# A hybrid mixer layer on one core: the last 512 columns of the second token tile in two halves, epsilon as a summand, the last stores over two queues

## The chip, the cores and the metric

The kernel runs on one core of a Trainium2 chip. What is measured is the device time of one execution in microseconds (us). The engines are named as in the profile: PE does the matrix products (PEld is its weight load), DVE the elementwise work on tensors, ACT the activations, POOL is the general-purpose engine, and SP issues transfers. A "q" behind a name (SPq, ACTq) marks what the engine's sequencer does, such as issuing a transfer.

## The reference

One layer on 256 tokens of 2048 features, all in float32. What matters here is its end:

```python
    gate = jax.nn.sigmoid(rmsnorm(x, ple_norm_g[i]) @ w_ple_gate[i])
    x = x + gate * (p[i] @ w_ple_proj[i])

return rmsnorm(x, final_norm_g)
```

with `rmsnorm(x, g) = x * rsqrt(mean(x * x) + EPS) * g` over the 2048 features of a token. Before it come the projection of the normalised input into ten fields, a short convolution and a gated recurrence on them, their merge, and an output projection that is added to x. The final norm needs the squares of all 2048 features of a token before any of them can be written.

## The kernel before

**Products.** Every weight matrix comes as a stream of chunks of 256 rows by 512 columns. SP loads them (L104), ACT rounds each to a first part (L117) and DVE subtracts to get the rest (L118), so that three products (L796 to L798) make up one of float32's accuracy. A group is 512 output columns; PE goes through its k tiles of 128 rows, and for each through both tiles of 128 tokens (`NT` = 2). The result of a group and a token tile fills one PSUM bank of 128 x 512.

**Order.** One list of steps (`steps`) gives the order of the chunks. After each step `advance()` moves every open epilogue, a Python generator, to its next `yield`; so the code of an epilogue stands in program order between the products of later steps. Each engine works through its own instructions in order, and a scheduler may set independent neighbours differently: of two halves, the two sigmoids come before the two squares on ACT. Semaphores carry the waits between engines. The last eight groups alternate between the per-layer embedding (`PP`, 2 k tiles) and the gate (`PG`, 16 k tiles), ending with a gate group. `ep_pg` (L596) handles the first three gate groups: sigmoid on ACT, product and sum on DVE, then on ACT the square with its sum over the columns (`accum_out`) into a column of `ss3`; POOL multiplies the result by the final gain.

**The last group.** It is written out by hand (L853 to L867). By then all its chunks are split or nearly so, so it is done by token tiles: all 48 products of tile 0 (16 k tiles, three products each), then all 48 of tile 1. `ep_last` for tile 0 runs beside tile 1's products; `ep_last` for tile 1 runs after everything.

**`ep_last` (L616)** takes the bank's 512 columns in two halves of 256: sigmoid (L624), times the embedding's part (L627), sum into x (L630), square with its sum (L631, which ends with an instruction that reads the accumulator out). Then DVE adds up the five sums of the token tile (L635), divides by 2048 and adds epsilon (L159), and POOL raises to the power -1/2 (L163). The four groups of columns are then scaled, two on ACT (L643, columns 0 to 1023) and two on DVE (L645, L647), and SP issues a store of 256 KB for each as it is ready (L650).

At the end the program waits for the transfers and the engines (L938).

Of the kernel before, what the change touches and what calls it, by code (L numbers as in the profile page):

```python
# [17 lines left out]
T = 256          # tokens  # L18
NT = T // P      # token tiles
D = 2048  # L20
KT = D // P      # k tiles of D
DC = 1024        # conv width
DR = 1024        # recurrent width
NH = 8           # heads
CW = 512         # columns of a product group
# [5 lines left out]
SCAN = 64        # tokens between restarts of the running sum of log f  # L31
LEVELS = [128, 64, 32, 16, 8, 4]      # block sizes inside a 128-token tile; pairs come apart

# columns of W_in in the order in which they are computed, in groups of 512
# [4 lines left out]
# columns of the packed per-feature parameters  # L39
# [5 lines left out]
def hybrid_kernel(ctx, tc, xT, x, pT, prm, gfin, masks, w_in, w_a, w_b, w_o, w_pg, w_pp, out):  # L45
# [8 lines left out]
    # what lives for a part of the kernel: by name, the pool and what closes it  # L54
# [32 lines left out]
    # ---------------------------------------------------------------- weights  # L87
    # a weight [groups of 512 columns, P, chunks of two k tiles, 2 * CW] comes as a stream of chunks
    stream = []                   # (weights, group, chunk)
    loaded = {}                   # raw tiles by (id, group, pair of chunks)  # L90
    parts = {}                    # split tiles by position in the stream
# [30 lines left out]
    # -------------------------------------------------------------- constants  # L122
# [16 lines left out]
    def operand(pool, tag, n):  # L139
        """n k tiles of a stationary operand, x^T-like: [P, n, T] in two parts."""  # L140
        return tuple(pool.tile([P, n, T], F32R, tag=tag + x, bufs=1, name=nm(tag + x)) for x in "hl")

    def put(op, k, src, scale=None):
        """src (fp32, [P, n]) times a per-partition gain into k tiles of an operand, as two parts."""
        hi, lo = op[0][:, k, :], op[1][:, k, :]
        if scale is None:
            nc.scalar.activation(out=hi, in_=src, func=AF.Copy)
            nc.vector.tensor_tensor(out=lo, in0=src, in1=hi.bitcast(F32), op=ALU.subtract)
        else:
            nc.scalar.activation(out=hi, in_=src, func=AF.Identity, scale=scale)  # L150
            nc.vector.scalar_tensor_tensor(
                out=lo, in0=src, scalar=scale, in1=hi.bitcast(F32), op0=ALU.mult, op1=ALU.subtract
            )

    # ----------------------------------------------------------- small pieces
    def rsqrt_of(ss, n, width, tag):
        """(ss / width + EPS) ** -0.5 for [P, n]."""
        v = sc(n, tag + "v", 2)
        nc.vector.tensor_scalar(  # L159
            out=v, in0=ss, scalar1=1.0 / width, scalar2=EPS, op0=ALU.mult, op1=ALU.add  # L160
        )
        r = sc(n, tag + "r", 2)
        nc.gpsimd.tensor_tensor(out=r, in0=v, in1=mhalf[:, :n], op=ALU.pow)  # L163
        return r

    def transposed(src):
        """src [P, NT, 512] token-major -> two PSUM banks, each [P, 2, T] (two column tiles)."""
        banks = []
        for half in range(2):
            b = bank("s")  # L170
            for i in range(2):
                c = half * 2 + i
                for t in range(NT):
                    nc.tensor.transpose(  # L174
                        b[:, i * T + t * P : i * T + (t + 1) * P],
                        src[:, t * CW + c * P : t * CW + (c + 1) * P],
                        ident,
                    )
            banks.append(b)
        return banks  # L180

    # --------------------------------------------------- epilogues, GEMM 1
# [14 lines left out]
    def times(psum, other, dst):  # L197
        """dst = (psum * rstd) * other"""
# [7 lines left out]
    def segments(ap):  # L206
        """[P, 1024] -> [P, head, tile of 128 tokens, segment, SCAN]"""
        return ap.rearrange("p (h k s c) -> p h k s c", h=4, k=2, c=SCAN)

    def ep_f(j, psum):  # L210
# [24 lines left out]
        # running sum of log f by position: with its own token in tile 0 (in time's order), and  # L235
        # without it in tile 1 (in the reverse order), restarting every SCAN tokens
# [51 lines left out]
    def hgrn(j):  # L288
        """
        The recurrence of four heads as masked products A[s, t] of two tiles of 128 tokens. Tile 1 is in  # L290
        the reverse order of time, so that at every level the keys of tile 0 lie where the queries of
        tile 1 do: one product serves both, A of tile 0 above the diagonal and A of tile 1 below it.
        """
# [27 lines left out]
        def tiles(ap, B):  # L321
            """[P, 1024] -> [P, head, tile, block of B, half, B / 2]"""
            return ap.rearrange("p (h k n two c) -> p h k n two c", h=4, k=2, two=2, c=B // 2)

        def combine(e, B):
            """The keys and the queries of a level, scaled by e."""
# [13 lines left out]
        def level(B):  # L340
            """By the decay between each token and the middle of its block of B."""
# [15 lines left out]
        # from the end of a segment, y = b - its sum  # L357
# [17 lines left out]
        # between the two tiles of 128 tokens  # L375
# [13 lines left out]
        # pairs of tokens and each token with itself: f of the later one on its query, 1 / f on its key  # L389
# [75 lines left out]
    def ep_xa(j, psum):  # L465
# [7 lines left out]
        for h in range(2):  # L473
            for i in range(2):
# [9 lines left out]
                # tokens 0 .. 127 in time's order, then tokens 255 .. 128  # L484
# [46 lines left out]
    # --------------------------------------------------- epilogues, the rest  # L531
# [64 lines left out]
    def ep_pg(j, psum):  # L596
        xs, pw, gt = state["x"], state["pw", j], t4()
        junk = t4()
        for t in range(NT):
# [9 lines left out]
                accum_out=state["ss3"][:, t * 5 + j : t * 5 + j + 1],  # L609
# [6 lines left out]
    def ep_last(t, psum):  # L616
        """The last 512 columns of a tile of tokens, its norm and its way out."""
        xs, pw, ss = state["x"], state["pw", 3], state["ss3"]
        n = 256
        gt, junk = t4(), t4()  # L620
        for h in range(2):
            s = slice(h * n, (h + 1) * n)
            d = xs[:, t, 3 * CW + h * n : 3 * CW + (h + 1) * n]
            nc.scalar.activation(  # L624
                out=gt[:, s], in_=psum[:, s], func=AF.Sigmoid, scale=state["rstd2"][:, t : t + 1]
            )
            nc.vector.tensor_tensor(  # L627
                out=gt[:, s], in0=gt[:, s], in1=pw[:, t * CW + h * n : t * CW + (h + 1) * n], op=ALU.mult
            )
            nc.vector.tensor_tensor(out=d, in0=d, in1=gt[:, s], op=ALU.add)  # L630
            nc.scalar.activation(  # L631
                out=junk[:, s], in_=d, func=AF.Square, accum_out=ss[:, t * 5 + 3 + h : t * 5 + 4 + h]
            )
        tot = sc(1, "tot3", 2)
        nc.vector.tensor_reduce(  # L635
            out=tot, in_=ss[:, t * 5 : (t + 1) * 5], axis=mybir.AxisListType.X, op=ALU.add
        )
        r = rsqrt_of(tot, 1, D, "r3")
        for q in (0, 2, 3, 1):
# [10 lines left out]
            nc.sync.dma_start(out=out[:, t, s], in_=d)  # L650
        yield

    # ------------------------------------------------------------ the program
# [4 lines left out]
    groups = []                   # (kind, j, weights, group in it, operand's name)  # L658
# [17 lines left out]
    # x^T and the first weights, in the order in which they are needed  # L676
# [15 lines left out]
    # a busy tensor engine runs at its full clock by the time the data is there  # L692
# [10 lines left out]
    def add_squares(c):  # L703
        """Towards the norm of x: squares summed over the k tiles, and in norm_of_x over the partitions."""
# [23 lines left out]
    def begin():  # L728
        """The lower bound of the forget gate, and what is needed later."""
        # softmax over the layers (one), its running sum, less the first  # L730
# [17 lines left out]
    def second_part():  # L748
        """The mixer's temporaries go; m^T comes."""
# [6 lines left out]
    def third_part():  # L756
        """The branches' outputs go; the residual stream comes back."""
# [18 lines left out]
        state["ss3"] = sc(10, "ss3", 1)  # L776
# [12 lines left out]
    def ahead(pos):  # L789
        """How many chunks are split by the time that one is used: all of the last group's at its start."""  # L790
        return LEAD + min(max(pos - (last_group - 8), 0), 5)

    def product(psum, op, k, t, hi, lo, first, last):
        """Three products make up one of float32's accuracy."""
# [58 lines left out]
    # the last group by tiles of tokens: the first one's end overlaps the second one's products  # L853
    for t in range(NT):
        bk = bank("g")
        for c in range(len(steps) - last_group):
# [4 lines left out]
            for i in range(2):  # L861
                k = 2 * c + i
                s = slice(i * CW, (i + 1) * CW)
                product(bk, state["x1T"], k, t, hi[:, s], lo[:, s], k == 0, k == KT - 1)
            if c % 2:
                advance()
        active.append(ep_last(t, bk))  # L867
# [6 lines left out]
def _chunks(w):  # L874
    """[K, N] -> [N / 512, 128, K / 256, 2 * 512]: row (2 c + i) * 128 + p of a group at [p, c, i]."""
# [5 lines left out]
def _features(v):  # L881
    """[n * 128] -> [128, n]"""
# [3 lines left out]
def _level_masks():  # L886
    """The pairs of each level, for both tiles; all of them, by tile; the pairs left over, by tile."""
# [7 lines left out]
def _in_order(v):  # L895
    """[T, n]: the second tile of tokens reversed (its own inverse)."""
# [46 lines left out]
```

## Time and profile before

| What | us |
|---|---|
| Three runs | 865.38, 866.03, 867.37 |
| Median | 866.03 |
| Span of the profiled execution | 864.5 |
| Time of the profiled execution beside its span | not given by the page |
| PE busy | 847.6 |
| Tile 1's products, first start | 844.3 |
| Tile 1's sigmoid | 855.5 |
| First scaling of tile 1 | 859.1 |
| First and last issue of its stores | 859.6, 861.0 |

A row of the page's fifth part names a line, an engine, an operation, its output and inputs, the shape and how often; then the busy time and the mean of one in ns, and the idle time ahead of it with what ended most of it. In the timeline the first two numbers are the start from the span's beginning and the duration, both in us; instructions of one group that follow each other stand in one row (x2), and the bracket tells the idle time ahead and its cause. Products overlap in the array, so the distance between the starts of two, not their duration, is what one costs. The view by stretches gives, for each, its length, the busy time and count of PE, PEld, DVE, ACT and POOL, the granted clock of PE, the busy share of the 16 DMA engines (which can come out a little above 1) and the GB/s moved.

### The profile page before, as it was taken

What the parts mean: (1) busy time and instruction counts of PE and PEld (TensorE: products, weight loads), DVE (VectorE), ACT (ScalarE), POOL (GpSimd) and SP (SyncE); (2) the same over time, 40 slices, a digit from 0 to 9 for tenths busy, and PEclk for the clock granted to TensorE, in tenths of its full rate; (3) what the DMA queues carried; (4) which work ended last, traced back from release to release, by engine and by line L of the source; (5) the groups of instructions that cost most, each with busy time, mean ns of one, the idle gap of its engine ahead of it and who ended that gap; (6) DMA issues with size and microseconds to landing.
All of it is one profiled execution on the core that took longest, in us unless ns stands there. A gap on an engine that the chain in (4) does not pass through costs nothing.

```text
span 864.5 us, 9830 instructions
## 1 busy us (share of the span) xinstructions
PE 847.6 (98%) x3853; PEld 697.8 (81%) x3853; DVE 535.0 (62%) x613; ACT 423.7 (49%) x514; POOL 94.3 (11%) x81
## 2 busy tenths in 40 slices
PE   8799999999999999999999999999999999999995
PEld 5588888888888888888888888888888888888884
DVE  7684586986674586976546447446446555555572
ACT  7474474444654573444444443444443544455552
POOL 3310032302010041302001001001001000001110
PEclk9999999999999999999999999999999999999999
DMA  9455545454455455454555555554554955454542
GB/s 337 181 194 196 195 160 181 149 194 159 181 186 176 174 195 195 147 181 160 181 193 191 172 193 194 191 195 171 197 192 172 354 191 195 172 187 165 207 147 97
DMA packets 25390, 162.02 MB, mean 187 GB/s; under 512 B 2944, under 2 KB 2944, under 8 KB 7168
## 3 DMA queue, kind: packets, MB, share of 16 engines
q1 hardware_dynamic: 25200, 161.36, 52.7%
q8 instruction: 30, 0.49, 0.2%
q14 instruction: 16, 0.13, 0.0%
q10 hardware_dynamic: 144, 0.04, 0.0%
HBM read 159.29 MB, written 2.10 MB: 187 GB/s over the span
## 4 chain that ended last, share of the span: by engine, by line
PE 93%; issue 2%; ACT 2%; DMA 1%; POOL 0%; SPq 0%; DVE 0%; POOLq 0%; ACTq 0%
PE g L796 30%; PE g L798 30%; PE g L797 29%; PE s L306 1%; PE s L174 1%; ACT whi L117 1%; DMA raw<-in_w_in 1%; ACT xh L150 0%; PE s L414 0%; PE s L572 0%; ACT t L712 0%; PE s L425 0%; PE s L426 0%; PE s L427 0%; POOL r1r L163 0%
## 5 line engine op out<-in xcount | busy, mean ns | idle before, releaser
L118 DVE TENSOR_TENSOR wlo<-raw,whi 128x1024 fp32r<-128x1024 f32 (+1 forms) x294 | 373.3, 1275 | 273.2 <-ACT whi L117 272.9
L117 ACT ACTIVATE whi<-raw 128x1024 fp32r<-128x1024 f32 (+1 forms) x294 | 308.6, 1052 | 375.1 <-PE g L798 366.6
L796 PE MATMUL g<-whi,xh 128*128 128x512 f32 x896 | 355.8, 398 | 0.8 <-ACT whi L117 0.8
L797 PE MATMUL g<-wlo,xh 128*128 128x512 f32 x896 | 350.7, 391 | 5.3 <-DVE wlo L118 5.3
L798 PE MATMUL g<-whi,xl 128*128 128x512 f32 x896 | 352.2, 393 | 0.0
L797 PEld LDWEIGHTS g<-wlo,xh 128*128 128x128 f32 x896 | 169.0, 189 | 43.1 <-DVE wlo L118 7.3
L798 PEld LDWEIGHTS g<-whi,xl 128*128 128x128 f32 x896 | 168.9, 189 | 38.0
L796 PEld LDWEIGHTS g<-whi,xh 128*128 128x128 f32 x896 | 169.1, 189 | 35.9 <-ACT whi L117 2.2
L796 PE MATMUL g<-whi,mh 128*128 128x512 f32 x128 | 50.8, 397 | 0.0
L798 PE MATMUL g<-whi,ml 128*128 128x512 f32 x128 | 50.2, 392 | 0.0
L797 PE MATMUL g<-wlo,mh 128*128 128x512 f32 x128 | 49.8, 389 | 0.0
L544 POOL TENSOR_TENSOR gb<-ga,gb 128x1024 f32<-128x1024 f32 x4 | 9.6, 2406 | 259.9 <-DVE gb L543 259.9
L334 POOL TENSOR_TENSOR X<-t,kT 128x256 f32<-128x256 f32 x12 | 11.4, 952 | 170.9 <-ACT t L348 117.1
L798 PEld LDWEIGHTS g<-whi,ml 128*128 128x128 f32 x128 | 24.0, 188 | 5.6
L797 PEld LDWEIGHTS g<-wlo,mh 128*128 128x128 f32 x128 | 24.1, 188 | 5.1
L796 PEld LDWEIGHTS g<-whi,mh 128*128 128x128 f32 x128 | 24.1, 188 | 4.7
L796 PE MATMUL g<-whi,yaTh 128*128 128x512 f32 x64 | 24.9, 390 | 0.0
L798 PE MATMUL g<-whi,yaTl 128*128 128x512 f32 x64 | 24.9, 390 | 0.0
L797 PE MATMUL g<-wlo,yaTh 128*128 128x512 f32 x64 | 24.9, 389 | 0.0
L796 PE MATMUL g<-whi,ybTh 128*128 128x512 f32 x64 | 24.9, 389 | 0.0
L797 PE MATMUL g<-wlo,ybTh 128*128 128x512 f32 x64 | 24.9, 389 | 0.0
L798 PE MATMUL g<-whi,ybTl 128*128 128x512 f32 x64 | 24.9, 389 | 0.0
(155 smaller groups left out, 579.0 us busy)
## 6 DMA issues: line engine op xcount, KB each, us to landing
raw<-in_w_in SPq DMA_DIRECT2D x91, 1024.0 KB, 4.8
raw<-in_w_o SPq DMA_DIRECT2D x16, 1024.0 KB, 4.8
raw<-in_w_pg SPq DMA_DIRECT2D x16, 1024.0 KB, 4.8
raw<-in_w_a SPq DMA_DIRECT2D x8, 1024.0 KB, 5.0
raw<-in_w_b SPq DMA_DIRECT2D x8, 1024.0 KB, 5.0
raw<-in_w_in SPq DMA_DIRECT2D x9, 512.0 KB, 7.8
t<-in_xT SPq DMA_DIRECT2D x8, 256.0 KB, 7.5
xs<-in_x SPq DMA_DIRECT2D x2, 1024.0 KB, 8.7
```

Source lines behind the costliest of these rows:

```text
L117: nc.scalar.activation(out=hi[:, s], in_=src[:, s], func=AF.Copy)
L118: nc.vector.tensor_tensor(out=lo[:, s], in0=src[:, s], in1=hi[:, s].bitcast(F32), op=ALU.subtract)
L174: nc.tensor.transpose(b[:, i * T + t * P : i * T + (t + 1) * P], src[:, t * CW + c * P : t * CW + (c + 1) * P], ident,)
L306: nc.tensor.matmul(bk[:, s], X[:, 0, h, :], X[:, 1, h, :], start=True, stop=True)
L334: eng.tensor_tensor(out=xv[:, w, :, :, half, :], in0=ev[:, :, blk, :, half, :], in1=src[:, :, blk, :, half, :], op=ALU.mult,)
L544: nc.gpsimd.tensor_tensor(out=gb, in0=ga, in1=gb, op=ALU.add)
L796: nc.tensor.matmul(psum, oh, hi, start=first, stop=False)
L797: nc.tensor.matmul(psum, oh, lo, start=False, stop=False)
L798: nc.tensor.matmul(psum, ol, hi, start=False, stop=last)
```

## The change

The last group is done in three pieces instead of two: tile 0 with 512 columns, then tile 1 with columns 0 to 255 of the group over all 16 k tiles, then with columns 256 to 511. Each piece has a bank of its own. The epilogue of a half (`last_half`) is put behind that half's products, so tile 1's first half is dealt with in program order before the second half's products are through; the norm (`last_norm`) comes after both. The sigmoid's tile also takes the squares that nobody reads.

The division by 2048 goes into the squares, as the activation's input scale, in `ep_pg` and in `last_half`. Each token tile has six summands instead of five; the sixth is epsilon, written once by POOL. L159's instruction goes from this norm, and POOL takes the power of the sum itself. In program order the sixth summand is set in `third_part`; in the order that the scheduler makes of it, it stands among POOL's first instructions.

Of the last stores, the one of columns 512 to 1023 is issued by ACT, the other three by SP. The scalings are written in the order 2, 0, 3, 1 instead of 0, 2, 3, 1; the stores on SP stood in the order 2, 0, 3, 1 before already.

Up to the last group, the instructions of all engines keep their order, but for the setting of epsilon.

```diff
@@ ep_pg
             nc.scalar.activation(
                 out=junk[:, s], in_=d, func=AF.Square,
-                accum_out=state["ss3"][:, t * 5 + j : t * 5 + j + 1],
+                scale=D**-0.5, accum_out=state["ss3"][:, t * 6 + j : t * 6 + j + 1],
             )
@@
-    def ep_last(t, psum):
...
+    def last_half(t, h, psum):
+        xs, pw, ss, n = state["x"], state["pw", 3], state["ss3"], CW // 2
+        gt = t4()[:, :n]
+        d = xs[:, t, 3 * CW + h * n : 3 * CW + (h + 1) * n]
+        nc.scalar.activation(out=gt, in_=psum, func=AF.Sigmoid, scale=state["rstd2"][:, t : t + 1])
+        nc.vector.tensor_tensor(
+            out=gt, in0=gt, in1=pw[:, t * CW + h * n : t * CW + (h + 1) * n], op=ALU.mult
+        )
+        nc.vector.tensor_tensor(out=d, in0=d, in1=gt, op=ALU.add)
+        nc.scalar.activation(
+            out=gt, in_=d, func=AF.Square, scale=D**-0.5,
+            accum_out=ss[:, t * 6 + 3 + h : t * 6 + 4 + h],
+        )
+
+    def last_norm(t):
+        xs = state["x"]
+        tot, r = sc(1, "tot3", 2), sc(1, "r3", 2)
         nc.vector.tensor_reduce(
-            out=tot, in_=ss[:, t * 5 : (t + 1) * 5], axis=mybir.AxisListType.X, op=ALU.add
-        )
-        r = rsqrt_of(tot, 1, D, "r3")
-        for q in (0, 2, 3, 1):
+            out=tot, in_=state["ss3"][:, t * 6 : (t + 1) * 6], axis=mybir.AxisListType.X, op=ALU.add
+        )
+        nc.gpsimd.tensor_tensor(out=r, in0=tot, in1=mhalf[:, :1], op=ALU.pow)
+        for q in (2, 0, 3, 1):
...
-            nc.sync.dma_start(out=out[:, t, s], in_=d)
-        yield
+            (nc.scalar if q == 1 else nc.sync).dma_start(out=out[:, t, s], in_=d)
+
+    def ep_last(t, halves):
+        for h, psum in enumerate(halves):
+            last_half(t, h, psum)
+        last_norm(t)
+        yield
@@ third_part
-        state["ss3"] = sc(10, "ss3", 1)
+        state["ss3"] = sc(12, "ss3", 1)
+        nc.gpsimd.memset(state["ss3"].rearrange("p (t j) -> p t j", t=NT)[:, :, 5:6], EPS)
@@ the last group
-    for t in range(NT):
-        bk = bank("g")
-        for c in range(len(steps) - last_group):
+    nlast = len(steps) - last_group
+    for t, halves in ((0, (0, 1)), (1, (0,)), (1, (1,))):
+        bk, n = bank("g"), CW // 2
+        for c in range(nlast):
...
-                s = slice(i * CW, (i + 1) * CW)
-                product(bk, state["x1T"], k, t, hi[:, s], lo[:, s], k == 0, k == KT - 1)
+                s = slice(i * CW + halves[0] * n, i * CW + (halves[-1] + 1) * n)
+                product(bk[:, : len(halves) * n], state["x1T"], k, t, hi[:, s], lo[:, s], k == 0, k == KT - 1)
             if c % 2:
                 advance()
-        active.append(ep_last(t, bk))
+        if t == 0:
+            active.append(ep_last(t, [bk[:, h * n : (h + 1) * n] for h in halves]))
+        else:
+            last_half(t, halves[0], bk[:, :n])
+    last_norm(1)
     finish()
```

More of the change, by code (lines that the diff above doesn't have):

```diff
@@ L614, in ep_pg @@
             nc.gpsimd.tensor_tensor(out=d, in0=d, in1=state["gfin"][:, j * CW : (j + 1) * CW], op=ALU.mult)
-    def ep_last(t, psum):
[L618 to L625, printed above, removed]
-            )
[L627 to L634, printed above, removed]
+    def last_half(t, h, psum):
[14 more added lines that the diff above has]
+        tot, r = sc(1, "tot3", 2), sc(1, "r3", 2)
         nc.vector.tensor_reduce(
-            out=tot, in_=ss[:, t * 5 : (t + 1) * 5], axis=mybir.AxisListType.X, op=ALU.add
+            out=tot, in_=state["ss3"][:, t * 6 : (t + 1) * 6], axis=mybir.AxisListType.X, op=ALU.add
         )
-        r = rsqrt_of(tot, 1, D, "r3")
-        for q in (0, 2, 3, 1):
+        nc.gpsimd.tensor_tensor(out=r, in0=tot, in1=mhalf[:, :1], op=ALU.pow)
+        for q in (2, 0, 3, 1):
             s = slice(q * CW, (q + 1) * CW)
```

## The prediction

> **What bounds the kernel now.** The page of the profile comes first: its head, the busy time of each engine, and the shares of the chain of work that ended last.
>
> ```profile
> span 864.5 us, 9830 instructions
> PE 847.6 (98%) x3853; PEld 697.8 (81%) x3853; DVE 535.0 (62%) x613; ACT 423.7 (49%) x514; POOL 94.3 (11%) x81
> PE 93%; issue 2%; ACT 2%; DMA 1%; POOL 0%; SPq 0%; DVE 0%; POOLq 0%; ACTq 0%
> ```
>
> PE owns 93% of the chain, so nearly all of the time is products, and the change leaves all of them alone but the last 48. What it can win lies behind the last product, and what it can lose lies in those 48. The timeline of the end is therefore the second view; its columns are start and duration in us, engine, line, operation, tiles and shapes.
>
> ```profile
> 844.34 0.40 PE L796 MATMUL g<-whi,xh 128*128 128x512 f32 x1
> ...
> 855.08 0.39 PE L798 MATMUL g<-whi,xl 128*128 128x512 f32 x1
> 855.51 0.84 ACT L624 ACTIVATE t<-g,r2r 128x256 f32<-128x256 f32 x2 [6.02 <-PE g L798]
> 856.01 0.79 DVE L627 TENSOR_TENSOR t<-t,pw 128x256 f32<-128x256 f32 x2 [6.71 <-ACT t L624]
> 856.72 0.42 DVE L630 TENSOR_TENSOR xs<-xs,t 128x256 f32<-128x256 f32 x1
> 857.17 0.42 ACT L631 ACTIVATE t<-xs 128x256 f32<-128x256 f32 x1 [0.82 <-DVE xs L630]
> 857.50 0.19 ACT L631 ACTIVATION_READ_ACCUMULATOR t<-xs 128x1 f32 x1
> 857.59 0.40 ACT L631 ACTIVATE t<-xs 128x256 f32<-128x256 f32 x1
> 857.89 0.19 ACT L631 ACTIVATION_READ_ACCUMULATOR t<-xs 128x1 f32 x1
> 858.11 0.16 DVE L635 TENSOR_REDUCE tot<-ss 128x1 f32<-128x5 f32 x1 [0.64 <-ACT t L631]
> 858.30 0.15 DVE L159 TENSOR_SCALAR r3v<-tot 128x1 f32<-128x1 f32 x1
> 858.54 0.55 POOL L163 TENSOR_TENSOR r3r<-r3v,mhalf 128x1 f32<-128x1 f32 x1 [10.42 <-DVE r3v L159]
> 859.12 1.33 ACT L643 ACTIVATE xs<-xs,r3r 128x512 f32<-128x512 f32 x2 [1.04 <-POOL r3r L163]
> 859.13 0.49 DVE L645 TENSOR_SCALAR xs<-xs,r3r 128x512 f32<-128x512 f32 x1 [0.67 <-POOL r3r L163]
> 859.64 0.33 SPq L650 DMA_DIRECT2D out<-xs  x1
> ...
> 861.04 0.40 SPq L650 DMA_DIRECT2D out<-xs  x1
> ```
>
> Three stretches follow each other. Token tile 1's 48 products run from 844.34 to the sigmoid at 855.51: 47 steps of (855.08 - 844.34) / 47 = 0.2285 us, then 0.43 from the last start to the sigmoid, 11.17 us together. From the sigmoid to the first scaling at 859.12 is a chain of single instructions, 3.61 us. From there to the end of the span are 5.4 us of scaling, storing and closing. None of the three hides under another, so what each gains or loses adds up.
>
> **Part one: the products in halves.** 48 products of 512 columns become 96 of 256, each with its own weight load. The trace has no product of this kind with 256 columns. The nearest rows are the narrow float32 ones of earlier stages, each with the wide product after it.
>
> ```profile
> 37.57 0.51 PE L722 MATMUL s<-ones,squares 128*128 128x8 f32 x4
> 37.93 0.48 PE L796 MATMUL g<-whi,xh 128*128 128x512 f32 x1
> 38.25 0.39 PE L797 MATMUL g<-wlo,xh 128*128 128x512 f32 x1
> ```
>
> ```profile
> 119.96 1.06 PE L306 MATMUL s<-X 128*128 128x128 f32 x8
> 120.78 0.48 PE L796 MATMUL g<-whi,xh 128*128 128x512 f32 x1
> 121.09 0.40 PE L797 MATMUL g<-wlo,xh 128*128 128x512 f32 x1
> ```
>
> Taking off one wide step, four records of 8 columns cost 38.25 - 37.57 - 0.2285 = 0.45 us, and eight of 128 columns 121.09 - 119.96 - 0.2285 = 0.90: both 0.1125 us apiece. Sixteen times the columns cost nothing more, so this is a floor for a pair of load and product, and the stream runs beside it rather than after it. Call the step of a 256-column product c; the stretch is then 95 c plus 0.32 (0.43 less half a wide step of stream). If the floor decides, c = 0.1125 and the stretch is 11.01, 0.16 less than now. If half the columns take half the step, c = 0.114: 11.18, no change. The straight line between 128 columns (0.1125) and 512 (0.2285) is the other end: 0.1125 + 128/384 x 0.116 = 0.151, 14.68 us, a loss of 3.51. Floor and stream are almost equal at 256 columns, so neither hides much of the other's unevenness, and any part of the wide step that is paid per product is paid twice. I take **c = 0.120**, an estimate near the floor and the half, since the equal cost at 8 and 128 columns says that what is narrow is limited by one thing and not by a sum: 95 x 0.120 + 0.32 = 11.72, a loss of **0.55 us**.
>
> **Part two: the chain behind the last product.** Tile 1's first half has its sigmoid, product, sum and square while PE works on the second half: 48 c = 5.8 us of cover for about 1.9 us of work. One half is left at the end. By the rows above: sigmoid to product 0.50; product 0.42 and a hand-over of 0.03 (as from L635 to L159); sum 0.45 (856.72 to 857.17); square 0.33 until its accumulator is read; reading 0.19 and 0.03; reduction 0.16; hand-over to POOL 0.09 (858.45 to 858.54); the power 0.55; 0.03 to the scaling. That is 2.78 against 3.61, **0.83 us saved**: 0.26 where two sigmoids, products and sums interleaved, 0.39 for one square with its reading, 0.18 for L159, whose division and epsilon go into the square's scale and into a sixth summand. If the cover were gone, the 0.65 of the first two would return.
>
> The epsilon summands are two elements per partition, set by one POOL instruction. In the changed kernel's own order it stands among the first POOL instructions, not at the tail. Such a setting of a 128x1 tile takes 0.10 us:
>
> ```profile
> 0.24 0.10 POOL L932 MEMSET const-float32-0.0<- 128x1 f32 x1 [0.24 <-issue]
> ```
>
> POOL is 11% busy over the span, and that idle time hides it; uncovered it is 0.1 us. The scale in the squares of L607 and L631 adds no instruction: nothing. One tile for sigmoid and square instead of two adds no wait, since each half's steps already follow each other.
>
> **Part three: the stores.** SP issues the four last stores from 859.64 to 861.04; now it issues three, in the same order of readiness, and ACT the fourth as soon as its second scaling ends, 859.12 + 1.33 = 860.45, so about 0.5 us sooner. Whether that counts depends on the DMA engines, which the view by stretches shows (the last two columns are their busy share and GB/s).
>
> ```profile
> 860.00:860.50 0.50, 0.00 (x0) 0.00 (x0) 0.28 (x1) 0.46 (x1) 0.00 (x0) 1.00 0.08 29
> 860.50:861.00 0.50, 0.00 (x0) 0.00 (x0) 0.00 (x0) 0.00 (x0) 0.00 (x0) 0.79 1.02 377
> ...
> 862.50:863.00 0.50, 0.00 (x0) 0.00 (x0) 0.00 (x0) 0.00 (x0) 0.00 (x0) 0.50 1.04 385
> 863.00:863.50 0.50, 0.00 (x0) 0.00 (x0) 0.00 (x0) 0.00 (x0) 0.00 (x0) 0.50 0.47 172
> ```
>
> From the first byte on, all engines are full until the 1.05 MB are out: 1.05 MB at 385 GB/s is 2.7 us. A store that is issued sooner only queues longer, and the first one's issue does not move against the scaling. I take **zero**. The bounds: 0.49 saved if the last issue counts after all (861.04 less the third one's start on SP, 860.55), and a loss of 0.33 if a store from ACT lands as slowly as its only other transfer:
>
> ```profile
> 860.55 0.40 SPq L650 DMA_DIRECT2D out<-xs  x1
> prm_t<-in_prm ACTq DMA_DIRECT2D x1, 36.0 KB, 3.6
> out<-xs SPq DMA_DIRECT2D x8, 256.0 KB, 2.4
> ...
> DMA to landing us min/median/max: 2.0/2.4/2.7
> ```
>
> The 3.6 us set from 860.47 end at 864.07, the slowest of today's stores at 861.04 + 2.7 = 863.74. The Trainium skill has the same rule, against this edit: "Trainium Kernel Development and Optimization", section Key Constraints, says that transfers issued from SP, ACT and POOL share the same 16 engines, so a second issuer saves only the sequencer's issue time; the full shares above agree.
>
> ```profile
> 848.15 1.34 ACT L643 ACTIVATE xs<-xs,r3r 128x512 f32<-128x512 f32 x2 [1.04 <-POOL r3r L163]
> ```
>
> In tile 0 the store on ACT stands ahead of the first half's sigmoid in ACT's queue, with the square behind that and DVE's product waiting for it. It is issued when the second scaling ends, 848.15 + 1.34 = 849.49, takes some 0.4 as on SP, and that sigmoid is due near 844.34 + 48 x 0.12 + 0.3 = 850.4. Were it late, 5 us of products would still cover it.
>
> **The sum.** +0.55 - 0.83 + 0 = -0.28 us on a span of 864.5, so 864.2. The page gives no time beside the span; the median of the three runs, 866.03, lies 1.5 above it, and I leave that as it is: 866.03 - 0.28 = **865.8 us**.
>
> **Rivals.** *The halves are free.* c is the floor, 0.1125, and 0.16 is won instead of lost: 866.03 - 0.83 - 0.16 = 865.0. For it: 8 and 128 columns cost the same. Against: those are another operand type, and no row has stream and floor equal. The Trainium skill, "TensorE: Matmul & The Clock Gate", section Back-to-back issue gap, gives N/2.4 + 2.5 ns, 109 ns at 256 columns; by that estimate the stretch is 10.7 and the time 864.7, but the same rule gives 216 ns at 512 where this trace has 228.5. Chance 0.22.
>
> *The loads decide, and it is slower.* Each product now streams half as long, while its load lasts as before:
>
> ```profile
> L797 PEld LDWEIGHTS g<-wlo,xh 128*128 128x128 f32 x896 | 169.0, 189 | 43.1 <-DVE wlo L118 7.3
> L306 PEld LDWEIGHTS s<-X 128*128 128x128 f32 x112 | 14.7, 192 | 1.2
> ```
>
> If a load must be through before its product may start and the next load waits for that start, c = 0.189: 18.28 us, a loss of 7.11, and 872.3 in all; at the line's 0.151 it is 868.7. The place is the step between two products of tile 1; the time is worse than before by over 0.2% (1.73 us) from c = 0.141 on, since 95 x 0.141 + 0.32 = 13.72 is 2.55 more than now, less 0.83. For it: PEld is 81% busy already. Against: L306's loads last 192 ns and yet follow each other every 112. Chance 0.16.
>
> *The second queue shortens the stores.* 0.49 more is saved: 865.3. Against it stand the full engines. Chance 0.07.
>
> **How the numbers follow.** The forecast, c from 0.116 to 0.14 with idle gains at the stores, has 0.55 and gives 865.4 to 867.7, all within 0.2% of before, which is about what a measurement of this kernel can tell from no change. The free halves stay within it too, unless the stores gain as well (-1.48 us) and the scatter of runs (865.38 to 867.37) helps: faster 0.10. Slower is the load rival with a little of the forecast's upper edge: 0.17. Within: 0.73. The range starts at that -1.48 with 0.25 for scatter, 864.3, and reaches past c = 0.141 to 868.2; beyond it lies most of the slow rival.
>
> **What the profile after would show.** The starts of tile 1's products give c directly: about 0.12, 0.1125 for the free case, over 0.14 for the slow one. One sigmoid, product, sum and square stand between the last product and the reduction; no L159 follows it; sigmoid to scaling is 2.8 us. DMA is full from 0.8 us after the first store's issue for 2.7 us, whichever engine issues. The prediction is wrong if c leaves 0.11 to 0.14, if the first half's steps lie behind the last product, or if the span after the scaling shrinks by half a microsecond.

## The result, and where the time went

The changed kernel takes 876.66 us (875.91 to 877.31, four runs) against 866.68 (865.38 to 867.37, four runs): the ratio is 1.0120, with a 95% interval of 1.0105 to 1.0134. It is slower by 10 us; the forecast was 865.8, in a range that ended at 868.2. The profiled execution of after took 875.91 us, with a span of 874.1.

The page of after, first part and chain:

```profile
span 874.1 us, 9924 instructions
PE 858.6 (98%) x3901; PEld 702.1 (80%) x3901; DVE 535.0 (61%) x611; ACT 424.3 (49%) x514; POOL 95.7 (11%) x82
...
PE 93%; issue 2%; ACT 2%; DMA 1%; POOL 1%; SPq 0%; DVE 0%; POOLq 0%; ACTq 0%
```

The shares are those of before; what grew is PE's busy time, by 11.0 us. The 48 extra products of the change (3901 against 3853) are in the last group. But the timeline of the end shows that the loss had happened ahead of it:

```profile
854.22 0.28 PE L803 MATMUL g<-whi,xh 128*128 128x256 f32 x1
...
865.58 0.28 PE L805 MATMUL g<-whi,xl 128*128 128x256 f32 x1
865.90 0.47 ACT L621 ACTIVATE t<-g,r2r 128x256 f32<-128x256 f32 x1 [3.79 <-PE g L805]
866.41 0.42 DVE L622 TENSOR_TENSOR t<-t,pw 128x256 f32<-128x256 f32 x1 [4.84 <-ACT t L621]
866.87 0.43 DVE L625 TENSOR_TENSOR xs<-xs,t 128x256 f32<-128x256 f32 x1
867.33 0.42 ACT L626 ACTIVATE t<-xs 128x256 f32<-128x256 f32 x1 [0.95 <-DVE xs L625]
867.65 0.19 ACT L626 ACTIVATION_READ_ACCUMULATOR t<-xs 128x1 f32 x1
867.87 0.16 DVE L635 TENSOR_REDUCE tot<-ss 128x1 f32<-128x6 f32 x1 [0.57 <-ACT t L626]
868.10 0.55 POOL L638 TENSOR_TENSOR r<-tot,mhalf 128x1 f32<-128x1 f32 x1 [10.29 <-DVE tot L635]
868.69 1.33 ACT L643 ACTIVATE xs<-xs,r 128x512 f32<-128x512 f32 x2 [0.86 <-POOL r L638]
...
869.21 1.30 SPq L650 DMA_DIRECT2D out<-xs  x3
870.06 0.36 ACTq L650 DMA_DIRECT2D out<-xs  x1
```

| Stretch | before, us | after, us | difference | predicted |
|---|---|---|---|---|
| to tile 1's first product | 844.34 | 854.22 | +9.88 | 0 |
| tile 1's products, to the sigmoid | 11.17 | 11.68 | +0.51 | +0.55 |
| sigmoid to scaling | 3.61 | 2.79 | -0.82 | -0.83 |
| scaling to the end of the span | 5.38 | 5.41 | +0.03 | 0 |

The three stretches that the prediction worked out came within 0.04 us each. What it held constant, the 844 us ahead of them, grew by 9.88.

Two views show what grew. The first is the view by stretches for 500 to 600 us, where the instructions of both kernels stand in the same order: before, then after.

```profile
500.00:600.00 100.00, 100.00 (x445) 82.48 (x444) 52.68 (x47) 42.88 (x44) 3.61 (x2) 1.00 0.55 189
```

```profile
500.00:600.00 100.00, 100.00 (x440) 81.78 (x439) 50.59 (x44) 42.75 (x44) 2.40 (x1) 1.00 0.55 190
```

PE is busy all the time in both, at a granted clock of 1.00, with the same DMA share; it just gets 440 products done instead of 445. From 40 us to tile 1 the same view counts 3688 products in both kernels, in 804 us before (40 to 844) and in 814 us after (40 to 854). The second view is the timeline of PE alone: two starts ten products apart in one group of x, in before and in after.

```profile
484.08 0.39 PE L797 MATMUL g<-wlo,xh 128*128 128x512 f32 x1
...
486.37 0.40 PE L798 MATMUL g<-whi,xl 128*128 128x512 f32 x1
```

```profile
454.96 0.39 PE L804 MATMUL g<-wlo,yaTh 128*128 128x512 f32 x1
...
457.23 0.39 PE L805 MATMUL g<-whi,yaTl 128*128 128x512 f32 x1
...
500.09 0.40 PE L804 MATMUL g<-wlo,xh 128*128 128x512 f32 x1
...
502.42 0.39 PE L805 MATMUL g<-whi,xl 128*128 128x512 f32 x1
```

Ten products of x cost 2.29 us before and 2.33 after; ten products of yaT (the second fence, first pair), the operand of another stage, cost 2.27 in after. Over all groups the mean step (the distance between the starts of neighbouring products) of x is 229.0 ns before and 232.5 after, that of m 232.4 after; that of yaT is 227.0 and 227.4. x and m are the stationary operand, the one that is loaded as weights while whi or wlo is streamed past it, in 3 x 896 - 48 + 3 x 128 = 3024 products ahead of tile 1, and 3024 x 3.5 ns = 10.6 us is about the loss of 9.88. Products that the change doesn't touch cost 3.5 ns more each, but those of x and m alone.

What tells x and m from yaT is where they lie in SBUF. The change removes L159's tile from this norm, which had two buffers of 32 bytes in the pool `small`. The tiles of `small` lie between the streamed weight tiles and x, so x, m and what follows on that side move down by 64 bytes in each partition; the streamed tiles (`whi`, `wlo`) and yaT stay. In the built programs the start addresses, modulo 256, are:

| | x, m | whi, wlo | yaT |
|---|---|---|---|
| before | 160 | 224 | 224 |
| after | 96 | 224 | 224 |

**Theory A:** the step of a product depends on how its stationary tile lies to the streamed tile, modulo some power of two. **Rival B:** the changed instructions or their order slow the products, wherever the tiles lie. With d for the start of the stationary tile less that of the streamed one, modulo 256: yaT has d = 0, x has 192 before (64 below the streamed tile) and 128 after.

### The profile page after: what moved, and what is told of

Its sections match the earlier page's. It is cut to its first block, busy times and chain, and to the rows that moved or that the text cites. A ratio compares the mean times of both kernels' runs of the same rounds, so it can differ in the third digit from the quotient of the medians.

```text
span 874.1 us, 9924 instructions
## 1 busy us (share of the span) xinstructions
PE 858.6 (98%) x3901; PEld 702.1 (80%) x3901; DVE 535.0 (61%) x611; ACT 424.3 (49%) x514; POOL 95.7 (11%) x82
## 4 chain that ended last, share of the span: by engine, by line
PE 93%; issue 2%; ACT 2%; DMA 1%; POOL 1%; SPq 0%; DVE 0%; POOLq 0%; ACTq 0%
PE g L805 30%; PE g L803 30%; PE g L804 30%; PE s L306 1%; PE s L174 1%; DMA raw<-in_w_in 1%; ACT whi L117 1%; DMA prm_t<-in_prm 0%; PE s L414 0%; PE s L572 0%; ACT t L718 0%; ACT xh L150 0%; PE s L427 0%; PE s L426 0%; PE s L425 0%
## 5 line engine op out<-in xcount | busy, mean ns | idle before, releaser
L804 PE MATMUL g<-wlo,xh 128*128 128x512 f32 (+1 forms) x912 | 357.6, 392 | 5.0 <-DVE wlo L118 4.9
L803 PE MATMUL g<-whi,xh 128*128 128x512 f32 (+1 forms) x912 | 360.1, 395 | 0.5 <-ACT whi L117 0.5
L805 PE MATMUL g<-whi,xl 128*128 128x512 f32 (+1 forms) x912 | 357.3, 392 | 0.0
L804 PEld LDWEIGHTS g<-wlo,xh 128*128 128x128 f32 x912 | 172.7, 189 | 43.9 <-DVE wlo L118 6.5
L803 PEld LDWEIGHTS g<-whi,xh 128*128 128x128 f32 x912 | 172.7, 189 | 39.1 <-ACT whi L117 1.9
L805 PEld LDWEIGHTS g<-whi,xl 128*128 128x128 f32 x912 | 172.5, 189 | 38.8
```

What stands on the lines that cost most here:

```text
L803: nc.tensor.matmul(psum, oh, hi, start=first, stop=False)
L804: nc.tensor.matmul(psum, oh, lo, start=False, stop=False)
L805: nc.tensor.matmul(psum, ol, hi, start=False, stop=last)
```

## The experiments

Most kernels are the changed one with a tile that nobody uses, ahead of `gain`, so that what lies behind it moves; no instruction differs. The step is the mean distance between the starts of neighbouring 512-column products of one group, over all groups of that operand but the last group of the kernel, without the steps of over 0.3 us, in which PE waited.

| Kernel | x, m at | whi, wlo at | d of x | step x, ns | step yaT, ns | median us | ratio (95%) |
|---|---|---|---|---|---|---|---|
| before | 160 | 224 | 192 | 229.0 | 227.0 | 866.68 | |
| after | 96 | 224 | 128 | 232.5 | 227.4 | 876.66 | 1.0120 (1.0105 to 1.0134) |
| e1 | 160 | 224 | 192 | 229.0 | 227.0 | 866.01 | 0.9999 (0.9990 to 1.0008) |
| e2 | 96 | 224 | 128 | 232.4 | 227.4 | 876.40 | 1.0128 (1.0111 to 1.0145) |
| e3 | 224 | 224 | 0 | 226.9 | 226.7 | 859.25 | 0.9925 (0.9910 to 0.9940) |
| e4 | 160 | 32 | 128 | 233.1 | 228.9 (d 192) | 878.78 | 1.0152 (1.0137 to 1.0167) |
| e5 | 224 | 224 | 0 | 226.9 | 226.7 | 859.91 | 0.9925 (0.9911 to 0.9938) |
| e6 | 224 | 224 | 0 | 227.0 | 226.7 | 859.65 | 0.9927 (0.9915 to 0.9940) |
| e7 | 224 | 224 | 0 | 226.9 | 226.7 | 859.42 | 0.9920 (0.9908 to 0.9932) |
| e8 | 96 | 224 | 128 | 232.5 | 227.4 | 876.02 | 1.0110 (1.0097 to 1.0124) |
| e9 | 32 | 224 | 64 | 233.4 | 227.3 | 878.75 | 1.0140 (1.0110 to 1.0169) |
| e10 | 192 | 224 | 224 | 233.3 | 227.0 | 878.99 | 1.0143 (1.0113 to 1.0172) |
| e11 | 0 | 224 | 32 | 233.3 | 226.8 | 877.89 | 1.0130 (1.0100 to 1.0159) |
| e12 | 224 | 224, 32 | 0, 192 | 232.0 | 231.9 | 876.12 | 1.0109 (1.0080 to 1.0139) |

Each ratio is against runs of before made beside it; e9 to e12 were timed twice each, the others four to ten times.

**e1: the change, with the addresses of before.**

```diff
+    small.tile([P, 16], F32, tag="pad", bufs=1, name="pad")
     def gain(base, k):
```

> The changed kernel, with 64 bytes per partition of unused filler in the pool of small tiles. The change took the two buffers of r3v away (64 bytes), so every tile laid out behind that pool on its side (the operands xh, xl, mh, ml and the last group's whi, wlo) moved down by 64 bytes; the filler puts all of them back to the addresses that they have in the kernel before. No instruction is added. Theory A (where the stationary operand lies sets PE's step): products with xh and mh fall from 232.5 to 229.0 ns, and the time to what the prediction's own terms gave, about 866.4 against 866.7 of before (ratio 0.9985 to 1.001). Rival B (something that the change does at run time slows every product: ACT's second transfer queue, POOL's setting of epsilon, other code): the step stays at 232.5 and the time at about 876.7.

Measured: 866.01 us beside 865.92 for before, ratio 0.9999. Ten steps of x in its timeline:

```profile
484.16 0.39 PE L807 MATMUL g<-whi,xl 128*128 128x512 f32 x1
...
486.45 0.39 PE L805 MATMUL g<-whi,xh 128*128 128x512 f32 x1
```

2.29 us, as before. All of the change's instructions are there and the 10 us are gone; rival B falls. And with equal addresses the change itself makes no measurable difference.

**e2: before, with the addresses of after.** The power is written over L159's result, so one tile less is kept.

```diff
-        r = sc(n, tag + "r", 2)
+        r = v if tag == "r3" else sc(n, tag + "r", 2)
```

> The kernel before, with one edit: the power of the last norm is written in place over r3v, so that the two buffers of r3r go and all that is laid out behind them moves down by the same 64 bytes as in the change. The instructions, their number and order stay. Theory A: the step of the xh and mh products rises from 229.0 to 232.5 ns, and the time by about 3050 x 3.5 ns = 10.7 us, to 877. Rival B: nothing moves, 866.7.

Measured: 876.40. Ten steps of x take 486.62 - 484.30 = 2.32 us:

```profile
484.30 0.39 PE L796 MATMUL g<-whi,xh 128*128 128x512 f32 x1
...
486.62 0.40 PE L797 MATMUL g<-wlo,xh 128*128 128x512 f32 x1
```

The loss comes without the change.

**e3: 64 bytes further up.** The filler of e1 with 32 elements instead of 16, so that x starts where the streamed tiles do, modulo 256.

```diff
+    small.tile([P, 32], F32, tag="pad", bufs=1, name="pad")
```

> The changed kernel with 128 bytes of filler: 64 beyond the addresses of before. xh then lies at 224 modulo 256, as whi and wlo do, and as yaT, ybT and pT do in all kernels, whose products take 227 ns. Theory A, with the residue modulo 256 (of the stationary operand itself or against the streamed one) as what counts: the step falls to 227.0, about 3050 x 2 ns = 6 us below the kernel before, about 860.5. If only the direction counted, nothing can be said; if the addresses of before were simply the good ones, 232 or more and 876. Rival B: 876.7.

Measured: 859.25, 0.9925 of before. Ten steps are 2.27 us, as those of yaT:

```profile
484.04 0.39 PE L805 MATMUL g<-whi,xh 128*128 128x512 f32 x1
...
486.31 0.39 PE L806 MATMUL g<-wlo,xh 128*128 128x512 f32 x1
```

So the address decides in both directions, and before had not the best one.

**e4: the streamed tiles moved as well.** The filler of e1, in the pool that lies ahead of the streamed tiles: x is back at 160, they are at 32.

```diff
+    const.tile([P, 16], F32, tag="pad", bufs=1, name="pad")
```

> The changed kernel with the 64 bytes of filler put ahead of the weight tiles as well: xh, mh stand at the addresses of before (160 modulo 256), but the streamed whi and wlo of all groups but the last move up by 64 (from 224 to 32 modulo 256), so that the distance between the two is what it is in the change. Theory A1 (the distance of stationary and streamed operand modulo 256 counts): xh at 232.5, and the yaT and ybT products, whose distance goes from 0 to 192, rise from 227 to 229; 877. Theory A2 (the address of the stationary operand alone counts): xh at 229.0, yaT and ybT stay at 227; 866.4.

Measured: 878.78. Its timeline has ten products of yaT, then ten of x:

```profile
456.65 0.39 PE L806 MATMUL g<-wlo,yaTh 128*128 128x512 f32 x1
...
458.94 0.39 PE L807 MATMUL g<-whi,yaTl 128*128 128x512 f32 x1
...
499.91 0.40 PE L806 MATMUL g<-wlo,xh 128*128 128x512 f32 x1
...
502.25 0.40 PE L807 MATMUL g<-whi,xl 128*128 128x512 f32 x1
```

2.34 us for x, though x lies where it lay before; 2.29 for yaT, which hasn't moved at all but now has d = 192, as x had in before. What counts is how the two tiles lie to each other, not where one of them is.

**e5: before, 64 bytes up.** The same filler as e1, put into before: x at 224 there too.

> The kernel before with nothing but 64 bytes of filler in the pool of small tiles, so that xh and mh lie at 224 modulo 256, at no distance from the streamed whi and wlo. If the distance is all that the change's layout did, this kernel gains what the third run gained: steps of 227 ns, and 859.4, as the change's own edits (0.6 lost on the narrower products, 0.8 won behind them) come to 0.2 us. If the change's edits themselves had won something larger that the layout hid, this one stays above 860.5.

Measured: 859.91, ratio 0.9925, the same as e3. At this layout too the change's own edits come to nothing that can be measured.

**e6: e3 with all last stores on SP.**

```diff
-            (nc.scalar if q == 1 else nc.sync).dma_start(out=out[:, t, s], in_=d)
+            nc.sync.dma_start(out=out[:, t, s], in_=d)
```

> The changed kernel with 128 bytes of filler and all last stores issued by SP, as before the change. The prediction's part three (full DMA engines, so the issuer costs nothing): 859.3, and in the trace the time from the first scaling to the span's end stays within 0.1 us of the third run's. If the second issuer had saved its 0.49 us, the span after the scaling grows by that: 859.8.

Measured: 859.65 beside 859.25 to 859.42 for e3 and e7, with intervals that overlap. The medians alone can't decide between the 859.3 and the 859.8 of the expectation; the traces can. The ends of e3, then of e6:

```profile
span 857.7 us, 9924 instructions
```

```profile
852.32 1.33 ACT L645 ACTIVATE xs<-xs,r 128x512 f32<-128x512 f32 x2 [0.86 <-POOL r L640]
...
852.83 1.30 SPq L652 DMA_DIRECT2D out<-xs  x3
853.68 0.36 ACTq L652 DMA_DIRECT2D out<-xs  x1
```

```profile
span 858.6 us, 9925 instructions
```

```profile
853.23 1.33 ACT L645 ACTIVATE xs<-xs,r 128x512 f32<-128x512 f32 x2 [0.86 <-POOL r L640]
...
853.75 1.80 SPq L652 DMA_DIRECT2D out<-xs  x4
```

From scaling to end are 857.7 - 852.32 = 5.38 us with two queues and 858.6 - 853.23 = 5.37 with one. With one queue the last issue ends 853.75 + 1.80 - 853.23 = 2.32 us behind the start of the scaling, with two 852.83 + 1.30 - 852.32 = 1.81, and nothing is gained by that.

**e7: e3 with tile 1 in one piece.**

```diff
-    for t, halves in ((0, (0, 1)), (1, (0,)), (1, (1,))):
+    for t, halves in ((0, (0, 1)), (1, (0, 1))):
...
-        if t == 0:
-            active.append(ep_last(t, [bk[:, h * n : (h + 1) * n] for h in halves]))
-        else:
-            last_half(t, halves[0], bk[:, :n])
-    last_norm(1)
+        active.append(ep_last(t, [bk[:, h * n : (h + 1) * n] for h in halves]))
```

> The changed kernel with 128 bytes of filler and token tile 1 in one piece again: 48 products of 512 columns, both halves of the epilogue behind them. Epsilon as a summand and the two queues stay. By the prediction's terms, at steps of 227 ns: 47 x 0.227 + 0.43 = 11.1 us of products against 95 x 0.1199 + 0.32 = 11.7, and a chain of about 3.43 us against 2.79: 859.25 within 0.1. If the halves were a clear gain it would be 859.9 or more, if a clear loss 858.6.

Measured: 859.42. Tile 1 in e3, then in e7:

```profile
837.82 0.28 PE L805 MATMUL g<-whi,xh 128*128 128x256 f32 x1
...
849.52 0.47 ACT L623 ACTIVATE t<-g,r2r 128x256 f32<-128x256 f32 x1 [3.82 <-PE g L807]
```

```profile
837.94 0.39 PE L805 MATMUL g<-whi,xh 128*128 128x512 f32 x1
...
849.02 0.84 ACT L623 ACTIVATE t<-g,r2r 128x256 f32<-128x256 f32 x2 [6.11 <-PE g L807]
...
852.45 1.33 ACT L645 ACTIVATE xs<-xs,r 128x512 f32<-128x512 f32 x2 [0.86 <-POOL r L640]
```

In halves: 11.70 us of products and 852.32 - 849.52 = 2.80 of chain, 14.50. In one piece: 11.08 and 3.43, 14.51. The halves give back in products what they save behind them. The time is 0.17 above that of e3 where 0.1 was allowed for; the runs of e7 spread from 858.60 to 860.53.

**e8: a full 256 bytes.** `small.tile([P, 64], ...)` as the filler: all addresses behind it are those of after plus 256.

> The changed kernel with 256 bytes of filler. If only the remainder modulo 256 of the distance between stationary and streamed operand counts, this is the changed kernel again: 128, steps of 232.5 ns, 876.7. If the addresses themselves or a longer period count, it is something else, such as 859 (any place further up is good) or a new value.

Measured: 876.02, step 232.5. The time of after is back, so of the shifts tried one of 256 bytes changes nothing. At d = 0 the built programs say the same: x of e3 starts 133 x 256 bytes behind the first streamed tile and yaT 568 x 256, an odd and an even multiple, and the steps are 226.9 and 226.7 ns.

**e9, e10, e11: other distances.** Fillers of 48, 24 and 40 elements.

> The changed kernel with 192 bytes of filler: xh and mh lie 64 above the streamed tiles modulo 256, where the layout of before has them 64 below. If only the size of the distance counts, steps of 229 ns and 866; if its direction counts, another value, up to the 232.5 ns and 876 of the distance 128.

> The changed kernel with 96 bytes of filler: xh and mh 32 below the streamed tiles modulo 256. If the cost grows evenly with the distance, 228 ns and 862.5; if a tile's place within 64 bytes matters too (all tiles so far lay at 32 modulo 64, these at 0), more than the 229 ns of the distance of 64.

> The changed kernel with 160 bytes of filler: xh and mh 32 above the streamed tiles modulo 256. Expected as for 32 below, 228 ns and 862.5, if only the size counts; with the ninth run it shows whether the two directions differ.

Measured: 233.4, 233.3 and 233.3 ns, 878 to 879 us. Ten steps of x in e9:

```profile
500.15 0.39 PE L807 MATMUL g<-whi,xl 128*128 128x512 f32 x1
...
502.49 0.39 PE L805 MATMUL g<-whi,xh 128*128 128x512 f32 x1
```

e9 lies even above the highest value that was expected for it (232.5 ns, 876 us). The expectations of e10 and e11 missed: a distance of 32 either way costs as much as 128. Nor is the cost symmetric, since 64 above costs 6.4 ns and 64 below 2. There is one good distance, zero, one nearly good one, and four bad ones; a cost that grows with distance does not fit. Distances of 96 and 160 weren't run. In e10 and e11, x also stands at another place within 64 bytes than in all other runs, and these two runs don't tell that from the distance.

**e12: one of the two streamed tiles moved.** `wlo` goes up by 64 bytes and x as well, so `whi` and x stand at 224 and `wlo` at 32.

```diff
-            parts[pos] = tuple(
-                pool.tile([P, 2 * CW], F32R, tag=tag, bufs=n, name=nm(tag)) for tag in ("whi", "wlo")
-            )
+            hi = pool.tile([P, 2 * CW], F32R, tag="whi", bufs=n, name=nm("whi"))
+            if pos == 0:
+                wp.tile([P, 16], F32, tag="padw", bufs=1, name="padw")
+            parts[pos] = hi, pool.tile([P, 2 * CW], F32R, tag="wlo", bufs=n, name=nm("wlo"))
...
+    small.tile([P, 16], F32, tag="pad", bufs=1, name="pad")
```

> The changed kernel with xh and mh at 224 modulo 256 as in the third run, whi there too, but wlo alone moved up by 64 (to 32) by a filler between the two. If a load and the product that streams at that time are what meets, only the step that begins with a product of wlo changes, by 1 to 4 ns, the two others stay at 227, and the time is 859 to 863. If it is rather the writes and reads of ACT and DVE on these tiles that disturb PE, all three steps change alike. If the distance to wlo counts as much as in the kernel before, all come to 229 and the time to 866.

Measured: 876.12. Ten products of yaT:

```profile
455.04 0.40 PE L808 MATMUL g<-whi,yaTl 128*128 128x512 f32 x1
...
457.35 0.40 PE L806 MATMUL g<-whi,yaTh 128*128 128x512 f32 x1
```

2.31 us, where yaT has 2.27 in after and 2.29 in e4 with both streamed tiles at 32. The expectation missed: not one step in three became longer but all three, and a mixture of d = 0 (227.0) and d = 192 (228.9) costs more (231.9) than either alone. So the step isn't set by the pair of tiles of that product alone. That all three change alike was expected if ACT and DVE disturbed PE. But in e12 the steps of x and m are 232.4 ns while neither of the two works (140 steps), and 232.0 and 231.7 beside ACT and beside DVE; so it isn't they. e12 is also the only run in which the two streamed tiles differ from each other modulo 256.

## Why the prediction was wrong

**The step that failed** is the first: "nearly all of the time is products, and the change leaves all of them alone but the last 48". Their instructions and their order it does leave alone. Their addresses it doesn't: two buffers of 32 bytes less in `small` move x and m by 64 bytes, from 64 below the streamed tiles' place modulo 256 to 128 away, and each of some 3000 products costs 3.5 ns more. e1 takes the shift back and the loss is gone; e2 makes the shift alone and the loss is there. The end of the kernel, on which all the prediction's rivals stood, had no part in it.

**Products in halves:** right. c = (865.58 - 854.22) / 95 = 0.1196 against 0.120, the stretch 11.68 against 11.72. The free halves (0.1125) and the loads that decide (0.189) are both refuted. In the layout of e3, where the wide step is 227, the halves cost 0.62 against e7. That c came out at the very value is partly luck: 0.120 was picked between 0.114 and 0.151, and of its two reasons the unevenness isn't seen, for in e3 nearly every step of the halves is 120 ns. A part that is paid per product whatever its width fits: 2 x 119.9 - 226.9 = 12.9 ns, an estimate by a straight line through two widths.

**The chain:** right, 2.79 us against 2.78, and 0.82 saved against 0.83. One sigmoid, one product, one sum and one square stand behind the last product, and L159 is gone. The first half's steps are covered: its sigmoid starts at 860.17, 5.7 us ahead of the second half's. The setting of epsilon (L783) takes 0.12 us at 6.0 us, off the path.

**The stores:** right at zero. ACT issues at 870.06, and SP's third issue ends at 870.51. The view by stretches of after (the DMA engines' share and GB/s stand last):

```profile
870.00:870.50 0.50, 0.00 (x0) 0.00 (x0) 0.00 (x0) 0.03 (x1) 0.00 (x0) 1.00 0.93 340
870.50:871.00 0.50, 0.00 (x0) 0.00 (x0) 0.00 (x0) 0.00 (x0) 0.00 (x0) 0.98 1.04 381
...
872.50:873.00 0.50, 0.00 (x0) 0.00 (x0) 0.00 (x0) 0.00 (x0) 0.00 (x0) 0.50 0.66 234
```

All engines are full from just after 870.0 until the data is out, as before; e6 shows the same from the other side. The second queue as a gain is refuted.

**The sum** of the change's own edits was -0.28 us; what the table of stretches gives without its first row is 0.51 - 0.82 + 0.03 = -0.28. With equal layouts (e1, and e3 beside e5) that is below what runs can tell, as forecast. The prediction was right about the edits and wrong about the kernel.

## What to carry to other kernels

When a change adds, drops or resizes any tile, however small, compare the start addresses of all tiles before and after, as one compares the order of instructions; to measure an edit, hold the layout with a filler of the size that went. Where products of 512 columns stream one tile against another all the time, try their starts at the same remainder modulo 256 bytes: here that was worth 0.75% (e5, ratio 0.9925), for one unused tile of 64 bytes in each partition, and the layouts other than these two cost 1.1 to 1.5%. It isn't a rule for all widths: products of 256 columns gained nothing by it (below).

## What the runs showed of the hardware

**The step of a product depends on the addresses.** For 512 columns it is 227 ns at d = 0, 229 at 192, and 232 to 233.4 at 32, 64, 128 and 224, at a mean granted clock between 0.992 and 0.996 in all of these runs. One kernel shows that no single address is good or bad in itself. The last group of after begins with streamed tiles at 224 and goes on, from the thirteenth product, with tiles of a pool that moves with x and stands at 96, as x does:

```profile
843.22 0.40 PE L803 MATMUL g<-whi,xh 128*128 128x512 f32 x1
...
845.55 0.39 PE L804 MATMUL g<-wlo,xh 128*128 128x512 f32 x1
...
849.91 0.39 PE L805 MATMUL g<-whi,xl 128*128 128x512 f32 x1
...
852.18 0.39 PE L803 MATMUL g<-whi,xh 128*128 128x512 f32 x1
```

Ten steps are 2.33 us at first and 2.27 later: 96 against 96 is as quick as 224 against 224.

**It lingers.** At a change from x to yaT in after (515.2 us), single steps still are 235, 233, 236, 224, 231, 236, 228, 233 and 231 ns before they settle at 226 to 227; at other such changes of after it takes one to nine steps. In e3, where both operands stand at d = 0, the same change (505.1 us) shows steps of 226 and 227 ns only. At a change from ybT to x (469.7 us) the last step of ybT is already long, and its stream runs beside the first load of x.

The Trainium skill, "TensorE: Matmul & The Clock Gate", section "Step-by-step: what each phase is for", says that PE reads the streamed operand and the weights of the next load over two independent ports, so that a load takes no bandwidth from a running product. The runs here differ: with the same instructions, the same products take up to 2.8% longer (233.4 against 227) by where the loaded tile lies to the streamed one. The measurement decides against it as a rule for every layout; at d = 0 it may hold, and that it is the load that takes the time is argued below, not shown.

**PE alone is enough for it.** Beside the work of other engines the step stays what it is. In before the steps of x and m are 229.0 ns while neither ACT nor DVE works (97 steps), 228.6 beside ACT alone and 228.9 beside DVE alone; in after they are 232.1 (138 steps), 232.5 and 232.4. In 50 steps of after in which neither ACT, DVE nor POOL works and no DMA engine moves a byte, they are 231.9. So neither the writes of ACT and DVE into these tiles nor transfers make the difference. That PE's own loads and streams meet in SBUF on something that repeats every 256 bytes fits this, the last step of ybT and the lingering, but no run shows it directly. Open are which reads meet, why 64 below costs only 2 ns, and why a mixture (e12) costs more than its parts.

**Products of 256 columns** don't follow the rule. Their mean step is 119.6 ns in after and e1 and 119.9 in e3, 6 to 7 ns over the 112.5 that narrower pairs cost and over half of the wide step of 227. But these means say little of d, for the tiles that the last group streams from its thirteenth product on move with x, so that d is 0 there in every run. Only the first twelve products of each half have the d of the table. Where d is 0, nearly every step is 120 ns; the first twelve have means from 115.0 to 119.7 ns in the runs with another d. The lowest is that of the second half in e9 (d = 64), whose wide step is the longest of all:

```profile
862.36 0.28 PE L807 MATMUL g<-whi,xl 128*128 128x256 f32 x1
...
863.50 0.28 PE L805 MATMUL g<-whi,xh 128*128 128x256 f32 x1
```

Ten steps take 1.14 us, against 1.20 in e3 (842.85 to 844.05). Equal remainders, the best layout for 512 columns, are here at best no better than the others. Twelve products in a half are few, and those before them may still linger.
